# The sum of a row's two magnitudes, ahead of the reciprocal that narrows x, made by GpSimd and not by VectorE

## The chip, the cores and the metric

One NeuronCore of a Trainium2 chip runs the whole program. The metric is the device time of one execution in microseconds (us). Three timed runs of the kernel before gave 1456.22, 1456.29 and 1456.98; the median is 1456.29.

## What is computed

```python
cs = np.cumsum(x, axis=1)                      # x: 8 x 2048 x 2048, float32
diff = cs - (cs shifted by one row, zeros first)
return np.matmul(diff, w).astype(np.float32)   # w: 2048 x 2048, float32
```

The differences of the running sums are x again, so the kernel computes x w: 16384 rows of x, each 2048 long, by a 2048 x 2048 matrix.

## The kernel before

The 16384 rows are cut into 128 tiles of 128 rows. The first four tiles (0 to 3) are multiplied plainly in bf16 while the weights are still coming in (L275, matmuls into eight PSUM banks, one for each row tile and 512 columns). All the others are multiplied in f16 by fewer products than the plain way: x and w are cut into quadrants, sums and differences of quadrants are formed by VectorE, and seven products of half the size take the place of eight. Tiles 4 to 7 use one level of this (`group_plain`), tiles 8 to 11 use two levels in part (`group_half`), and 29 groups of four tiles use two levels, in an order written out by hand (`ORDER`), whose entries name a step and the group that it belongs to. Every engine has its own queue and works it off in the order in which the program was recorded: `after(engine, ...)` keeps the recorded order on each engine. An instruction that waits holds up all that stands behind it on its engine.

So that f16 can be used, every row of x is scaled by its own size, and every product is scaled back. For each of the 124 tiles t from 4 on the steps are:

- `load`: SP fetches the tile in two halves into F.
- `weigh` (L123, ScalarE): for each half the sum of |x| / 4000 along the row goes to column 0 or 1 of a small tile `of` (128 x 8). In the profile this is an ACTIVATE with a following ACTIVATION_READ_ACCUMULATOR, which delivers the sum.
- `scale_of`: column 2, m = max(sum 0 + sum 1, TINY) (L139, VectorE), then column 3, s = 1 / m (L141, VectorE).
- `unit_of` (L147, GpSimd): column 4, u = m times uw, where uw is the scale of the weights. It is used much later, when products are written out.
- `narrow` (L158, ScalarE): x times s to f16, for each half.
- `turn` (L171, SP): a transposing DMA of each half into the tiles x, which TensorE loads as stationary operand.

The products leave PSUM through `keep` (L581, ScalarE) and `add` (L584, VectorE), both scaled by u. VectorE forms the sums of quadrants of x (L544) and of w (L382, L457, L536, L541, L937).

At the head of the program, when the last weights are in, comes this: VectorE forms the largest |w| of each partition (L366), GpSimd reduces that over the partitions (L367, a PARTITION_ALL_REDUCE), and then GpSimd issues seven output DMAs of the plain rows (L285). VectorE turns the result into the weights' scale (L369, L371) and begins to scale the weights to f16: `block(B11, ...)`, `block(B21, ...)`, `block(B12, ...)`, one L382 for each of 8 pieces. Between these blocks stand the `scale_of` of tiles 4, 6 and 5:

```python
for k in range(4):
    block(B11, 0, 0, k, "dve")
weigh(PLAIN); scale_of(PLAIN); unit_of(PLAIN)      # tile 4
for k in range(4, KH):
    block(B11, 0, 0, k, "dve")
narrow(PLAIN); turn(PLAIN); finish_row(0)
for k in range(4):
    block(B21, 1, 0, k, "dve")
weigh(PLAIN + 2); scale_of(PLAIN + 2); unit_of(PLAIN + 2)
finish_row(1)
```

`finish_row(r)` gives TensorE the last plain matmuls of row tile r (L275) and ScalarE the two copies out of its PSUM banks (L295). After the plain rows TensorE does one product that was left over, in the bank that the first copy of row tile 1 empties (`left_over(bank(2))`, L400, 16 matmuls, with all of B11 and B21), and then the products of tiles 4 to 7 (L554).

Of the kernel before, what the change touches and what calls it, by code (L numbers as in the profile page):

```python
# [10 lines left out]
def kernel(  # L11
# [6 lines left out]
    nc = tc.nc  # L18
# [12 lines left out]
    ADD = mybir.AluOpType.add  # L31
    SUB = mybir.AluOpType.subtract
    MUL = mybir.AluOpType.mult
    MAX = mybir.AluOpType.max
# [5 lines left out]
    TINY = 1e-34  # L40
# [45 lines left out]
    def after(engine, ask):  # L86
        if engine in last:
            with tc.issue_after(last[engine].ins):
                said = ask()
        else:  # L90
            said = ask()
        last[engine] = said[-1] if isinstance(said, tuple) else said
        return said
# [38 lines left out]
    def scale_of(t):  # L132
        if t < END:
            m2 = sums_of.pop(t)
            m, s, u = (m2[:, i : i + 1] for i in (2, 3, 4))
            scales[t], unit[t] = s, u
            after(
                "dve",
                lambda: nc.vector.tensor_scalar(m, m2[:, :1], m2[:, 1:2], TINY, ADD, MAX),  # L139
            )  # L140
            after("dve", lambda: nc.vector.reciprocal(s, m))  # L141
            sizes[t] = m
# [37 lines left out]
    with ExitStack() as head:  # L180
# [232 lines left out]
        for k in range(4):  # L413
            block(B11, 0, 0, k, "dve")
        weigh(PLAIN)
        scale_of(PLAIN)
        unit_of(PLAIN)
        for k in range(4, KH):
# [4 lines left out]
        for k in range(4):  # L423
            block(B21, 1, 0, k, "dve")
        weigh(PLAIN + 2)
        scale_of(PLAIN + 2)
        unit_of(PLAIN + 2)
        finish_row(1)
# [15 lines left out]
        for k in range(5, KH):  # L444
            block(B12, 0, 1, k, "dve")
        scale_of(PLAIN + 1)
        unit_of(PLAIN + 1)
        narrow(PLAIN + 1)
# [837 lines left out]
```

## Time and profile before

| | |
|---|---|
| median of three timed runs | 1456.29 us |
| profiled execution: its span, first to last instruction | 1455.0 us |
| instructions | 20120 |
| busy: TensorE / VectorE / ScalarE / GpSimd | 1441.1 / 1333.3 / 967.5 / 48.6 us |
| L139 on VectorE | 124 times, 206 ns each |
| L141 on VectorE | 124 times, 164 ns each |
| L147 on GpSimd | 124 times, 281 to 1896 ns, mean 370 |

The span is that of one profiled execution. The page gives no other time of that execution; the median of the runs stands 1.3 us above the span. Engines are named PE (TensorE's matmuls), PEld (its weight loads), DVE (VectorE), ACT (ScalarE), POOL (GpSimd) and SP (the engine that issues most DMAs). In a row of the timeline stand the start in us from the span's start, the time in us, the engine, line and operation, output and inputs, how many instructions the row merges, and in square brackets how long the engine was idle before and what ended that. In a row of groups the number before the bar is the count, and behind it stand the busy time and the mean ns of one.

### The profile page before, as it was taken

To read this page: it belongs to the slowest core of one execution; us is meant where nothing else is said; L and a number is where in the kernel's file an instruction comes from. 1 tells how busy PE (TensorE), PEld (TensorE's weight loads), DVE (VectorE), ACT (ScalarE), POOL (GpSimd) and SP (SyncE) were. 2 spreads that over 40 slices of the span, in tenths; PEclk is the share of its full clock that TensorE was granted. 3 is DMA by queue.
4 is the path that set the end of the run, shared out by engine and by line. 5 is a ranking of instruction groups with operands and counts; after the bars stand their busy time and mean duration, and the time that the engine had idled before them with its cause. 6 is when DMAs were issued, how large, how long until landed. Compare 5 with 4: busy or idle time off the path is not lost.

```text
span 1455.0 us, 20120 instructions
## 1 busy us (share of the span) xinstructions
PE 1441.1 (99%) x6673; PEld 652.6 (45%) x6679; DVE 1333.3 (92%) x2302; ACT 967.5 (66%) x1446; POOL 48.6 (3%) x136
## 2 busy tenths in 40 slices
PE   8999999999999999999999999999999999999998
PEld 3444444444444444444444444444444444444443
DVE  7998899999999999999999999999999999999998
ACT  5887656676666666667666667766666766666662
POOL 0111000000000000000000000000000000000000
PEclk9999999999999999999999999999999999999999
DMA  9999868898888998878998888998878898888983
GB/s 360 367 240 299 236 171 234 248 246 232 234 237 237 248 253 230 235 236 233 260 241 233 231 228 240 260 238 241 225 235 247 247 233 239 226 244 246 253 203 123
DMA packets 377752, 351.59 MB, mean 242 GB/s; under 512 B 274800, under 2 KB 274800, under 8 KB 377520
## 3 DMA queue, kind: packets, MB, share of 16 engines
q1 hardware_dynamic: 377088, 348.47, 84.9%
q0 software_dynamic: 560, 1.84, 0.3%
q8 instruction: 52, 0.85, 0.2%
q14 instruction: 52, 0.43, 0.1%
HBM read 150.99 MB, written 134.22 MB: 196 GB/s over the span
## 4 chain that ended last, share of the span: by engine, by line
PE 96%; DMA 2%; DVE 1%; issue 0%; ACT 0%; SPq 0%; DVEq 0%; ACTq 0%
PE b L573 61%; PE b L554 32%; PE b L275 2%; DMA W<-in_w_dram 1%; DMA W<-in_x_dram 1%; DVE c L584 1%; ACT wb L259 0%; PE b L400 0%; DVE x L544 0%; SPq L219 0%; DVE b L1030 0%; DVE flow L937 0%; DVE inner L544 0%; DVE W L541 0%; ACT c L581 0%
## 5 line engine op out<-in xcount | busy, mean ns | idle before, releaser
L584 DVE SCALAR_TENSOR_TENSOR c<-b,of,c 128x512 f32<-128x512 f32 x790 | 574.1, 747 | 74.3 <-PE b L573 64.3
L554 PE MATMUL b<-W,x 128*128 128x512 f16 x2144 | 506.6, 379 | 0.0
L581 ACT ACTIVATE c<-b,of 128x512 f32<-128x512 f32 x492 | 312.6, 680 | 230.9 <-PE b L573 113.3
L573 PE MATMUL b<-W,x 128*128 128x512 f16 x1892 | 452.4, 379 | 0.8 <-ACT b L1023 0.7
L158 ACT ACTIVATE F<-F,of 128x1024 f16<-128x1024 f32 x246 | 282.2, 1147 | 174.8 <-DVE of L141 172.6
L573 PEld LDWEIGHTS <-x 128*128 128x128 f16 x2488 | 243.4, 98 | 295.3 <-issue 2.7
L554 PEld LDWEIGHTS <-x 128*128 128x128 f16 x2144 | 209.8, 98 | 253.0 <-DVE x L544 0.2
L123 ACT ACTIVATE waste<-F 128x1024 uint8<-128x1024 f32 x246 | 259.3, 1054 | 4.6 <-DMA F<-in_x_dram 2.5
L573 PEld LDWEIGHTS <-inner 128*128 128x128 f16 x1648 | 161.2, 98 | 195.6 <-issue 1.3
L573 PE MATMUL b<-W,inner 128*128 128x512 f16 x944 | 242.2, 379 | 0.9 <-DVE b L1030 0.9
L544 DVE TENSOR_TENSOR x<-x,x 128x1024 f16<-128x1024 f16 (+1 forms) x388 | 226.6, 584 | 3.3
L573 PE MATMUL b<-flow,x 128*128 128x512 f16 x588 | 150.9, 379 | 0.0
L573 PE MATMUL b<-inner 128*128 128x512 f16 x472 | 121.1, 379 | 0.0
L937 DVE TENSOR_TENSOR flow<-W 128x2048 f16<-128x2048 f16 x87 | 105.8, 1216 | 0.0
L1030 DVE TENSOR_TENSOR b<-b,c 128x512 f32<-128x512 f32 x116 | 80.6, 695 | 13.9 <-PE b L573 13.9
L147 POOL TENSOR_SCALAR of<-of,uw 128x1 f32<-128x1 f32 x124 | 43.6, 370 | 1306.7 <-DVE of L139 704.1
L937 DVE TENSOR_TENSOR flow<-W,inner 128x2048 f16<-128x2048 f16 x58 | 70.8, 1220 | 0.0
L1023 ACT COPY c<-b 128x512 f32<-128x512 f32 x58 | 33.4, 576 | 51.3 <-PE b L573 51.3
L275 PE MATMUL b<-wb,xP 128*128 128x512 bf16 x234 | 57.0, 395 | 5.3 <-ACT wb L259 3.9
L544 DVE TENSOR_TENSOR inner<-x 128x512 f16<-128x512 f16 x117 | 49.4, 422 | 2.9 <-DMA x<-F 0.9
L1023 ACT COPY b<-b 128x512 f32<-128x512 f32 x87 | 51.2, 588 | 0.5 <-PE b L573 0.5
L544 DVE TENSOR_TENSOR inner<-x,inner 128x512 f16<-128x512 f16 x117 | 49.2, 421 | 2.0
(67 smaller groups left out, 530.0 us busy)
## 6 DMA issues: line engine op xcount, KB each, us to landing
F<-in_x_dram SPq DMA_DIRECT2D x246, 512.0 KB, 5.1
out_dram<-c SPq DMA_DIRECT2D x492, 256.0 KB, 3.0
W<-in_w_dram SPq DMA_DIRECT2D x32, 512.0 KB, 9.6
W<-in_x_dram SPq DMA_DIRECT2D x16, 256.0 KB, 7.2
x<-F SPq DMA_TRANSPOSE x246, 3.4
out_dram<-o POOLq DMA_DIRECT2D x5, 256.0 KB, 4.1
out_dram<-o SPq DMA_DIRECT2D x5, 256.0 KB, 3.5
xP<-in_x_dram SPq DMA_DIRECT2D x1, 1024.0 KB, 5.1
```

The costliest lines, as they stand in the source:

```text
L123: lambda: nc.scalar.activation(waste, where[t][i], ABS, scale=1.0 / ROW, accum_out=sums_of[t][:, i : i + 1],),
L147: after("pool", lambda: nc.gpsimd.tensor_scalar(u, m, uw, None, MUL))
L158: lambda: nc.scalar.activation(narrowed(t)[:, ds(i * NH, NH)], where[t][i], COPY, scale=s),
L275: lambda: nc.tensor.matmul(ps[r][n], xP[:, r, ko, :], wb[h, ko][:, ds(n * NB, NB)], start=(ko == 0), stop=(ko == KO - 1),),
L544: after("dve", lambda: nc.vector.tensor_tensor(dst.all, p.all, q.all, op))
L554: said = nc.tensor.matmul(to[n], a[k], b[k][:, n, :], start=(first and k == 0), stop=(k == KH - 1), skip_group_check=True,)
L573: said = nc.tensor.matmul(to, a[k], b[k], start=(first and k == 0), stop=(k == 3), skip_group_check=True)
L581: after("act", lambda: nc.scalar.activation(c, p, COPY, scale=u))
L584: after("dve", lambda: nc.vector.scalar_tensor_tensor(c, p, u, c, MUL, ADD))
L937: after("dve", lambda: nc.vector.tensor_tensor(in_twos(flow), x, y, op))
L1023: after("act", lambda: nc.scalar.copy(c, p))
L1030: after("dve", lambda: nc.vector.tensor_tensor(t, p, s, ADD))
```

## The change

L139 goes from VectorE's queue to GpSimd's. What it computes, its operands and its place in the program are the same.

```diff
             after(
-                "dve",
-                lambda: nc.vector.tensor_scalar(m, m2[:, :1], m2[:, 1:2], TINY, ADD, MAX),
+                "pool",
+                lambda: nc.gpsimd.tensor_scalar(m, m2[:, :1], m2[:, 1:2], TINY, ADD, MAX),
             )
             after("dve", lambda: nc.vector.reciprocal(s, m))
```

GpSimd's queue at the head, behind the output DMAs of the plain rows (`o`). The ISA row is the pair that the profile names MODIFY_POOL_CONFIG; `of` is the small tile of sums and scales.

```order
 L285 DMA out_dram<-o_120 128x512
 L285 DMA out_dram<-o_124 128x512
-L147 ISA
-L147 TENSOR_SCALAR of<-of,uw 128x1 x124
+L139 ISA
+L139 TENSOR_SCALAR of<-of 128x1
+L147 TENSOR_SCALAR of<-of,uw 128x1
```

The configuration and the first L139 stand where the configuration and the first L147 stood, behind the seven DMAs. Before, the first L147 waited for VectorE's L139; now L139 waits for ScalarE's sums, and L147 for L139.

VectorE's queue at the same place, from the weights' scale on. W are the weights.

```order
 L371 RECIPROCAL uinv<-uw 128x1
 L382 TENSOR_SCALAR W<-W,uinv 128x2x512 x4
-L139 TENSOR_SCALAR of<-of 128x1
 L141 RECIPROCAL of<-of 128x1
 L382 TENSOR_SCALAR W<-W,uinv 128x2x512 x8
-L139 TENSOR_SCALAR of<-of 128x1
 L141 RECIPROCAL of<-of 128x1
 L382 TENSOR_SCALAR W<-W,uinv 128x2x512 x12
```

L139 is gone, and L141 stays where it was, with the scaling of the weights behind it; it now waits for GpSimd.

VectorE's queue in a regular group, at one of the four scales of a group; x and inner are quadrant sums of x.

```order
 L544 TENSOR_TENSOR x_69<-x_69,x_70 128x1024
 L544 TENSOR_TENSOR inner<-x_69 128x512
-L139 TENSOR_SCALAR of<-of 128x1
 L141 RECIPROCAL of<-of 128x1
 L544 TENSOR_TENSOR inner<-inner,x_67 128x512
```

Here too only L139 has left. The queues of TensorE, ScalarE and SP hold the same instructions in the same order.

## The prediction

> **What bounds the kernel now.** I read the page first: busy shares and the chain that ended last, then the costliest groups.
>
> ```profile
> span 1455.0 us, 20120 instructions
> PE 1441.1 (99%) x6673; PEld 652.6 (45%) x6679; DVE 1333.3 (92%) x2302; ACT 967.5 (66%) x1446; POOL 48.6 (3%) x136
> PE 96%; DMA 2%; DVE 1%; issue 0%; ACT 0%; SPq 0%; DVEq 0%; ACTq 0%
> ```
>
> TensorE is busy 1441.1 of 1455.0 us and is 96% of the chain. VectorE's 92% looks close behind, but it is an average. So the next view is the busy time by stretch: the stage in which the weights are turned (76 to 131), the first seven-product groups (131 to 197), and the regular groups.
>
> ```profile
> core 0: us, PE busy (x) PEld busy (x) DVE busy (x) ACT busy (x) POOL busy (x), PEclk, DMA share, GB/s
> 76.00:131.00 55.00, 55.00 (x256) 24.95 (x255) 50.73 (x84) 43.83 (x62) 5.97 (x6) 1.00 1.01 260
> 131.00:197.00 66.00, 64.38 (x296) 28.61 (x294) 58.14 (x95) 39.80 (x61) 5.45 (x4) 1.00 0.76 217
> 197.00:1450.00 1253.00, 1252.57 (x5803) 567.57 (x5801) 1161.10 (x2046) 827.81 (x1258) 29.94 (x112) 1.00 0.85 235
> ```
>
> Behind 197 us TensorE is idle for 0.43 us in all (1253.00 - 1252.57), from 131 to 197 for 1.6, from 76 to 131 for nothing. A microsecond taken from VectorE buys nothing there, and a microsecond by which TensorE is held up at the head is not made good later: it goes onto the end.
>
> **What is removed.** The grouped rows of the moved operation and of the operation that GpSimd does already:
>
> ```profile
> L139 DVE TENSOR_SCALAR of<-of 128x1 f32<-128x1 f32 x124 | 25.6, 206 | 3.4 <-ACT waste L123 3.3
> L147 POOL TENSOR_SCALAR of<-of,uw x124: 281/282/1896, 71.8 to 1414.0; 128x1 f32<-128x1 f32 x124
> L147 POOLq MODIFY_POOL_CONFIG  x2: 37/37/37, 64.1 to 64.1; - x2
> ```
>
> VectorE loses 124 x 0.206 = 25.6 us, but about 111 of the 124 lie behind 197 us (GpSimd's 112 operations in that row are L147, one to each L139), beside a full TensorE. I count them at 0. The limit of the gain is the idle time of TensorE above, 2.0 us, and its stalls there are round trips through VectorE and ScalarE that no L139 lies in; I take nothing of it.
>
> **What is added in the regular groups.** One L139 goes to GpSimd for each row tile, and L141 on VectorE then waits for GpSimd. GpSimd's queue ahead of it holds only L139 and L147 of earlier tiles, so it starts when ScalarE's second sum is read out. The tightest such place in a group of 44 us:
>
> ```profile
> 760.89 0.20 ACT L123 ACTIVATION_READ_ACCUMULATOR waste<-F 128x1 f32 x1
> 763.37 0.21 DVE L139 TENSOR_SCALAR of<-of 128x1 f32<-128x1 f32 x1
> ```
>
> The sums are there at 761.09; VectorE comes to this place at 763.37. GpSimd has 2.28 us, and the longest one-column operation that it shows is 1.90. L141 finds its operand there: 0. If that cover were gone (an L139 of 2.6 us), VectorE would wait some 0.3 us, less than it has won.
>
> **What is added at the head.** Here it is another matter. The timeline of the first scale and what hangs on it:
>
> ```profile
> 59.51 1.48 POOL L285 DMA_DIRECT2D out_dram<-F  x2
> 60.98 3.05 POOL L285 DMA_DIRECT2D out_dram<-o  x5
> ...
> 63.40 0.19 ACT L123 ACTIVATION_READ_ACCUMULATOR waste<-F 128x1 f32 x1
> 63.62 0.21 DVE L139 TENSOR_SCALAR of<-of 128x1 f32<-128x1 f32 x1 [0.76 <-ACT waste L123]
> 63.87 0.16 DVE L141 RECIPROCAL of<-of 128x1 f32<-128x1 f32 x1
> 63.95 5.38 DVE L382 TENSOR_SCALAR W<-W,uinv 128x1024 f16<-128x1024 f32 x8
> 64.06 2.33 ACT L158 ACTIVATE F<-F,of 128x1024 f16<-128x1024 f32 x2 [0.48 <-DVE of L141]
> 65.24 2.75 SPq L171 DMA_TRANSPOSE x<-F  x2
> 66.95 1.07 ACT L295 COPY wb<-b 128x512 f32<-128x512 f32 x2 [0.56 <-PE b L275]
> ...
> 70.06 0.18 ACT L123 ACTIVATION_READ_ACCUMULATOR waste<-F 128x1 f32 x1
> 70.16 0.56 ACT L295 COPY wb<-b 128x512 f32<-128x512 f32 x1
> 70.28 0.21 DVE L139 TENSOR_SCALAR of<-of 128x1 f32<-128x1 f32 x1 [0.96 <-ACT waste L123]
> ...
> 70.61 8.03 DVE L382 TENSOR_SCALAR W<-W,uinv 128x1024 f16<-128x1024 f32 x12
> ...
> 71.80 2.26 POOL L147 TENSOR_SCALAR of<-of,uw 128x1 f32<-128x1 f32 x2 [7.77 <-DVE W L382]
> 72.15 3.62 PE L400 MATMUL b<-W,xP 128*128 128x512 f16 x16
> ```
>
> GpSimd's last output DMA is issued by 64.03. Its first one-column operation waits only for the first L139, over at 63.83, and yet starts at 71.80. Between them stand the two MODIFY_POOL_CONFIG at 64.1, which switch GpSimd from the all-reduce to its ordinary operations. The VectorE row printed as releaser cannot be the cause: this L147 reads neither W nor anything that L382 writes, and VectorE's own pause of 0.96 us ahead of 70.28 let nothing in. I read the 7.7 us as the price of the switch. Before the change nobody needs L147 until the first products are written out. After it the switch stands ahead of L139, and VectorE, ScalarE and TensorE stand behind it. Step by step:
>
> - First L139: starts at 71.80 and not at 63.62. Its time on GpSimd is not in the trace; the bounds are L147's 0.28 and 1.90. I take 0.28, since VectorE stands still and L147's long times lie beside a busy VectorE. With about 0.04 to hand over, L141 starts at 72.12: 8.25 us later.
> - Behind L141 on VectorE are eight L382 (second half of B11, first half of B21): 72.2 to 77.6. Behind the narrowing on ScalarE (L158, now from 72.31, 2.33 us, to 74.64) are the copies of row tile 0, the sums of the next x tile and the copies of row tile 1. From the copy at 66.95 to the one at 70.16 ScalarE needs 3.21 us without a pause; from 74.64 this gives 77.85, and with its 0.56 us 78.41. The pause of 0.56 ahead of 66.95 is used up.
> - That copy empties the PSUM bank into which L400 writes. L400 stands next in TensorE's queue, so nothing passes it: it starts at 78.41 and not at 72.15, **6.26 us later**.
> - What else L400 needs is there. The second L139 starts when the sums are read out at 77.94; L141 follows at 78.26, and the last four L382 of B21 come at 0.67 us each (8.03 / 12), from 79.0 to 81.0. L400 needs the first of them at its 13th matmul, 78.41 + 12 x 0.22 = 81.0 at the earliest. The transposes on SP wait for the narrowing and move by 8.3 us, to 76.3; the first product needs them at 81.9.
> - Later on VectorE runs 7.4 us late (8.25 less the pauses and three L139) against TensorE's 6.26. The supplies that arrived closest before had about 1.2 us to spare, so 0 more.
>
> **The clock of TensorE.** A pause of 6.1 us is longer than any in this trace, but two places show what pauses do. First the start, where the PEclk column has no record and the matmul rows have to be read, and then the end:
>
> ```profile
> 12.47 4.45 PE L275 MATMUL b<-wb,xP 128*128 128x512 bf16 x10 [0.78 <-DVE xP L247]
> 17.57 1.99 PE L275 MATMUL b<-wb,xP 128*128 128x512 bf16 x6
> ...
> 1449.00:1450.00 1.00, 0.57 (x3) 1.00 0.71 264
> 1451.00:1452.00 1.00, 0.00 (x0) 0.89 0.86 324
> 1452.00:1453.00 1.00, 0.00 (x0) 0.50 0.36 137
> ```
>
> The ten matmuls from 12.47 come every 0.43 us, the sixteen of L400 every 0.22; the change falls into the row of 17.57, near 18.2. And after the last matmul (1449.57) the granted clock is 0.50 from 1451.8 on: 2.2 us of idleness do it. So after 6.1 us TensorE restarts at half speed. The nearest price is the start's: 12.47 to 18.2 = 5.7 us at half speed, of which half, **2.8 us**, is lost. Bounds: 0 (the clock holds) and 4.6 (half speed as long as from the first of these matmuls, 9.0 to 18.2).
>
> The Trainium skill, "TensorE: Matmul & The Clock Gate", Part 1, has the clock watched in free-running windows of 3.4 us, halved after an idle window and restored after a busy one; by it the loss would be an estimated 1.7 to 3.4 us, and the drop after 2.2 us here agrees only if a window that is partly idle counts.
>
> **Sum.** Against the profiled execution: 1455.0 + 6.26 + 2.8 = 1464.1 us of span. The median of the runs, 1456.29, stands 1.3 above the span; with it, 1465.4.
>
> The Trainium skill, "GPSIMD Engine Reference", section 2.1, gives about 6 us (5.95) for the load of code at the first call after a MODIFY_POOL_CONFIG; the row here has 7.7, which I use, and with 5.95 the sum would be 1463.7.
>
> **Rivals.**
> - **No switch to wait for (not slower).** The 7.7 us were something that held L147 alone (VectorE's L382 blocking GpSimd, say), and L139 runs at once at 64.1. For it: the page's releaser, and twelve long L147 at the head. Then L141 starts at 64.5, 0.6 us late; ScalarE's pause of 0.56 takes that in, L400 still waits for its own turn at 72.15, and the time is 1456.2. It decides if the first L139 ends before about 65.8: the copy that L400 needs was over at 70.72, 1.4 us early, and with the pause that makes 2 us of cover. Against it: GpSimd stayed idle in VectorE's pause.
> - **The switch without the clock.** Half speed is not entered or is left at once: 1456.3 + 6.3 = 1462.6. Against it: 2.2 us sufficed at the end.
> - **Dearer head.** The first L139 takes 1.9 us, and half speed lasts as at its worst: 1465.4 + 1.6 + 1.8 = 1468.8. For it: L147's first two times are long.
> - **Faster.** VectorE's 25.6 us shorten TensorE's stalls behind 76 us: at most 2.0 us, 1454.3, and only together with the first rival.
>
> **How the numbers follow.** The forecast, 0.70; switch without clock, 0.12; dearer head, 0.06; no switch, 0.10; faster, 0.02. A measurement of this kernel tells 0.2% (2.9 us) from no change. Slower is 0.70 + 0.12 + 0.06 = 0.88, same 0.10, faster 0.02. The range takes in both clock cases and most of the dearer head, and something for a switch that is quicker while VectorE and SP stand still: 1461.0 to 1468.5.
>
> **What would show it.** In the profile after: MODIFY_POOL_CONFIG at 64.1 under L139; the first L139 near 71.8; L141 idle before for some 9 us on GpSimd; L400 near 78.4 with ScalarE's L295 as releaser; L400's mean well over 379 ns, and PEclk 0.5 for a few us behind 75; and from 200 us on the same 44 us per group, with everything shifted by one constant. A first L139 at 64.2 proves the first step wrong; L400's matmuls at 379 ns, the clock's; a shift that grows along the groups, the claim that the regular part costs nothing.

## The result and the profile after

The changed kernel takes 1465.33 us (median of 4 runs, 1464.81 to 1466.29); the kernel before, run beside it, 1456.26 (1456.07 to 1456.98). The ratio is 1.0061 with a 95% interval of 1.0047 to 1.0075: slower by 9.1 us, where 1465.4 was forecast.

The span of the profiled execution is 1463.6 us. Its page:

```profile
span 1463.6 us, 20203 instructions
PE 1441.1 (98%) x6673; PEld 652.1 (45%) x6679; DVE 1311.2 (90%) x2178; ACT 969.9 (66%) x1446; POOL 158.1 (11%) x260
```

TensorE's busy time adds up to the same 1441.1 us, VectorE has 22 us less to do, GpSimd 110 more, and the span has grown by 8.6. That TensorE's two sums agree is chance, since slow matmuls count as busy: up to 72.2 us the profile after has 63.1 us of busy time and the one before 65.3, and the slow matmuls of L400 then add 2.4. Where the 8.6 us lie, the timeline of the head shows:

```profile
63.18 0.19 ACT L123 ACTIVATION_READ_ACCUMULATOR waste<-F 128x1 f32 x1
71.99 0.31 POOL L139 TENSOR_SCALAR of<-of 128x1 f32<-128x1 f32 x1 [7.96 <-issue]
72.34 0.16 DVE L141 RECIPROCAL of<-of 128x1 f32<-128x1 f32 x1 [9.48 <-POOL of L139]
72.42 5.37 DVE L382 TENSOR_SCALAR W<-W,uinv 128x1024 f16<-128x1024 f32 x8
72.54 2.33 ACT L158 ACTIVATE F<-F,of 128x1024 f16<-128x1024 f32 x2 [9.17 <-DVE of L141]
...
77.96 0.56 ACT L295 COPY wb<-b 128x512 f32<-128x512 f32 x1
78.15 0.30 POOL L139 TENSOR_SCALAR of<-of 128x1 f32<-128x1 f32 x1 [4.90 <-ACT waste L123]
78.48 0.17 DVE L141 RECIPROCAL of<-of 128x1 f32<-128x1 f32 x1 [0.69 <-POOL of L139]
78.58 6.00 PE L400 MATMUL b<-W,xP 128*128 128x512 f16 x16 [6.49 <-ACT wb L295]
```

The configuration of GpSimd now stands under L139:

```profile
L139 POOLq MODIFY_POOL_CONFIG  x2: 37/37/37, 64.1 to 64.1; - x2
```

The sums are ready at 63.37, and the first L139 starts 8.6 us later, with "issue" as the reason for GpSimd's pause: nothing that the profile records was missing. VectorE waits 9.48 us for it, ScalarE 9.17 us for VectorE, and L400 6.49 us for the copy that empties its bank. L400 itself then needs 6.00 us for the 16 matmuls that took 3.62.

The windows around the restart give the clock (columns: stretch, its length, PE busy, granted clock, DMA share, GB/s), and those behind it, with all engines, what became of the rest (shifted by the 8.8 us of the head):

```profile
75.00:78.00 3.00, 0.00 (x0) 0.77 1.19 207
78.00:83.00 5.00, 4.42 (x11) 0.50 0.89 288
83.00:84.00 1.00, 1.00 (x6) 0.78 0.95 357
84.00:85.00 1.00, 1.00 (x6) 1.00 1.23 298
```
```profile
84.80:139.80 55.00, 55.00 (x256) 24.95 (x255) 49.03 (x77) 42.81 (x60) 9.96 (x12) 1.00 0.97 254
139.80:205.80 66.00, 64.43 (x296) 28.69 (x294) 57.33 (x91) 40.15 (x61) 5.88 (x10) 1.00 0.76 217
205.80:1458.00 1252.20, 1252.20 (x5802) 567.49 (x5800) 1140.40 (x1933) 829.90 (x1258) 134.74 (x223) 1.00 0.86 235
```

TensorE restarts at half clock and has its full clock back within the slice from 83 to 84. From 84.8 on every stretch is what it was: 55.00 of 55.00 busy, then 64.43 of 66 (64.38 before), then a full TensorE. The loss lies wholly ahead of 85 us. In the chain the first product of tile 4 (L554) begins at 84.58 and not at 75.76: 8.8 us.

### The profile page after: what moved, and what is told of

It reads as the page before. It is cut to its first block, busy times and chain, and to the rows that moved or that the text cites. A ratio compares the mean times of both kernels' runs of the same rounds, so it can differ in the third digit from the quotient of the medians.

```text
span 1463.6 us, 20203 instructions
## 1 busy us (share of the span) xinstructions
PE 1441.1 (98%) x6673; PEld 652.1 (45%) x6679; DVE 1311.2 (90%) x2178; ACT 969.9 (66%) x1446; POOL 158.1 (11%) x260
## 4 chain that ended last, share of the span: by engine, by line
PE 93%; DMA 4%; issue 1%; DVE 1%; ACT 0%; POOL 0%; SPq 0%; POOLq 0%; DVEq 0%
PE b L573 61%; PE b L554 33%; DMA W<-in_w_dram 2%; DMA W<-in_x_dram 2%; DVE c L584 1%; PE b L400 0%; POOL out_dram L285 0%; SPq L253 0%; SPq L219 0%; ACT wb L295 0%; ACT waste L123 0%; DVE wmax L262 0%; ACT F L158 0%; DVE b L1030 0%; ACT c L581 0%
## 5 line engine op out<-in xcount | busy, mean ns | idle before, releaser
L554 PE MATMUL b<-W,x 128*128 128x512 f16 x2144 | 506.6, 379 | 0.0
L554 PEld LDWEIGHTS <-x 128*128 128x128 f16 x2144 | 209.7, 98 | 253.0 <-DVE x L544 0.2
L139 POOL TENSOR_SCALAR of<-of 128x1 f32<-128x1 f32 x124 | 96.8, 780 | 1198.4 <-ACT waste L123 1190.5
L147 POOL TENSOR_SCALAR of<-of,uw 128x1 f32<-128x1 f32 x124 | 57.2, 473 | 3.7
L544 DVE TENSOR_TENSOR inner<-inner,x 128x512 f16<-128x512 f16 x117 | 49.5, 423 | 2.1
```

What stands on the lines that cost most here:

```text
L139: lambda: nc.gpsimd.tensor_scalar(m, m2[:, :1], m2[:, 1:2], TINY, ADD, MAX),
L147: after("pool", lambda: nc.gpsimd.tensor_scalar(u, m, uw, None, MUL))
L544: after("dve", lambda: nc.vector.tensor_tensor(dst.all, p.all, q.all, op))
L554: said = nc.tensor.matmul(to[n], a[k], b[k][:, n, :], start=(first and k == 0), stop=(k == KH - 1), skip_group_check=True,)
```

## The experiments

Two theories were in question beside the forecast. The **switch theory** is the forecast's: the reconfiguration of GpSimd behind the all-reduce holds its first ordinary operation for 7.7 us. The **output DMA theory** says that GpSimd is still at work on the seven DMAs that it issued. The **hand-over theory** says that every reciprocal now waits a little for GpSimd, 124 times. Each kernel is told by its difference from the changed one; its line numbers can be up to 17 higher, or one lower.

### Only the first L139 on GpSimd

```diff
-            after("pool", lambda: nc.gpsimd.tensor_scalar(m, ...))
+            name, by = ("pool", nc.gpsimd) if t == PLAIN else ("dve", nc.vector)
+            after(name, lambda: by.tensor_scalar(m, ...))
```

> Only the first row tile's L139 (tile 4) is on GpSimd, the other 123 stay on VectorE. Switch theory: the switch of GpSimd's configuration stands ahead of this one instruction and holds it to about 72 us, so the whole loss is there: first L139 near 72.0, L400 near 78.6 and at half speed, time 1465 (1464 to 1467). Rival, hand-over: each L139 on GpSimd costs the same small wait on its way to VectorE, so 1/124 of the 9 us is left: 1456.4.

Measured: 1465.22 us, ratio 1.0059 (1.0044 to 1.0074). One instruction of the 124 carries the whole loss. Its rows (the moved line is L140 here, L400 is L401):

```profile
72.48 0.31 POOL L140 TENSOR_SCALAR of<-of 128x1 f32<-128x1 f32 x1 [8.05 <-issue]
79.07 6.18 PE L401 MATMUL b<-W,xP 128*128 128x512 f16 x16 [7.15 <-ACT wb L296]
```

The hand-over theory would have left 0.1 us; it falls.

### All but the first on GpSimd

```diff
+            name, by = ("pool", nc.gpsimd) if t > PLAIN else ("dve", nc.vector)
...
```

> The first L139 is back on VectorE, the other 123 are on GpSimd. Switch theory: the switch now stands ahead of the first L147 and of the second L139, which is wanted at 70.3 and comes at about 72.5, so the second reciprocal is some 2 us late; the copy that L400 needs stands ahead of it in ScalarE's queue, and of the last four pieces of B21 the last is late by 0.3 us at most. L400 near 72.2 to 72.6, full speed, time 1456.0 to 1457.0. Rival, hand-over: 123/124 of the loss stays: 1465.

Measured: 1458.66 us, ratio 1.0016 (1.0007 to 1.0024): 2.1 us slower than the kernel before (1456.57), where 0 to 0.5 was expected. The mechanism was there, its size was not. The timeline (L400 is L401, L409 is L410, L554 is L555):

```profile
72.44 0.30 POOL L148 TENSOR_SCALAR of<-of,uw 128x1 f32<-128x1 f32 x1 [7.87 <-issue]
72.73 0.31 POOL L140 TENSOR_SCALAR of<-of 128x1 f32<-128x1 f32 x1
73.07 0.16 DVE L142 RECIPROCAL of<-of 128x1 f32<-128x1 f32 x1 [3.98 <-POOL of L140]
...
75.93 0.38 PE L401 MATMUL b<-W,xP 128*128 128x512 f16 x1 [0.29 <-DVE W L383]
...
84.53 6.20 PE L555 MATMUL b<-W,x 128*128 128x512 f16 x28 [0.45 <-ACT x L410]
```

The second reciprocal waits 3.98 us for the same switch and comes 2.5 us later than before. The gaps between matmul starts that were not there before add up to 2.1 us: 0.8 in L400 for the pieces of B21, 0.6 where a product waits for L400's bank to be emptied, 0.3 at the product with S1 and 0.4 at 98. I had counted the first of these alone. The agreement with 2.1 us is loose: the profiled span is 1.7 us longer than before (1456.7 for 1455.0).

### No switch

```diff
-        whole_max = nc.gpsimd.partition_all_reduce(uw, wred, P, bass_isa.ReduceOp.max)
+        whole_max = nc.gpsimd.tensor_scalar(uw, wred, TINY, None, MAX)
```

> The kernel after the change with the reduction over the partitions left out: GpSimd takes each partition's own largest weight with an ordinary one-column operation in its place, so that the weights' scale differs by partition and the output is not the product; everything else stays, the seven output DMAs ahead of the first L139 too. Switch theory: with no other kind of operation before it there is no switch at 64 us; the first L139 runs right behind the DMAs, near 64.1 to 64.4, L400 near 72.2 at full speed, time 1456 to 1457. Rival, output DMAs: GpSimd is still at work on the DMAs that it issued up to 64.0, their last packets go out at 67.3, and holds its next operation until 72: time stays at 1465.

Measured: 1456.76 us, ratio 1.0001 (0.9992 to 1.0010). There is no MODIFY_POOL_CONFIG at 64 us, and with all 124 L139 on GpSimd and all seven DMAs ahead of them the loss is gone:

```profile
60.68 3.06 POOL L285 DMA_DIRECT2D out_dram<-o  x5
...
63.77 0.32 POOL L139 TENSOR_SCALAR of<-of 128x1 f32<-128x1 f32 x1
64.12 0.16 DVE L141 RECIPROCAL of<-of 128x1 f32<-128x1 f32 x1 [1.57 <-POOL of L139]
...
71.93 3.62 PE L400 MATMUL b<-W,xP 128*128 128x512 f16 x16
```

L139 starts as soon as the last DMA is issued. The output DMA theory falls. The rival of the prediction in which VectorE's L382 block GpSimd falls by the changed kernel itself: there VectorE stood still for 9.48 us, and L139 did not start before 71.99.

### The switch begins sooner

```diff
-        with tc.issue_after(whole_max.ins):
-            for c, rows, columns in done:
-                put(c, rows, columns)
+        for c, rows, columns in done:
+            after("sp", lambda: put(c, rows, columns, nc.sync))
```

> The kernel after the change, with the seven output DMAs of the plain rows issued by SP and not by GpSimd, so that the switch begins right behind the all-reduce at 59.7 instead of 64.1. Switch theory: the first L139 starts near 67.5, 4.4 us sooner than in the kernel after; L400 near 74.2 instead of 72.1, a pause of some 2 us; with what VectorE and ScalarE are then behind, 1459.5 if TensorE keeps its clock over the shorter pause, up to 1461.5 if it does not. Rival, output DMAs: with no DMA work on GpSimd the first L139 runs at 63.4 and the time is 1456.3.

Measured: 1459.40 us, ratio 1.0020 (1.0011 to 1.0030); the lower end of what the switch theory expected.

```profile
L139 POOLq MODIFY_POOL_CONFIG  x2: 83/83/83, 59.0 to 59.0; - x2
```
```profile
66.59 0.31 POOL L139 TENSOR_SCALAR of<-of 128x1 f32<-128x1 f32 x1 [7.53 <-issue]
...
73.18 3.61 PE L399 MATMUL b<-W,xP 128*128 128x512 f16 x16 [1.59 <-ACT wb L295]
```

With no DMA of GpSimd's own in the way the switch still takes 7.5 us. It counts from the configuration and not from the all-reduce: in the changed kernel 4.4 us of DMA issue lie between the two, and the pause behind them is no shorter for it. TensorE's pause is now 1.6 us, and the 16 matmuls take 3.61 us: this pause does not cost the clock. The rest of the 3.0 us above the kernel before (1456.45) comes later, above all here, where TensorE waits for the copy that empties L400's bank (L409 is L408, L554 is L553):

```profile
84.53 7.07 PE L553 MATMUL b<-W,x 128*128 128x512 f16 x32 [0.83 <-ACT x L408]
```

### Two more switches

```diff
-                put(c, rows, columns)
+                last["pool"] = put(c, rows, columns)
+        after("pool", lambda: nc.gpsimd.tensor_scalar(idle[:, :1], wred, TINY, None, MAX))
+        after("pool", lambda: nc.gpsimd.partition_all_reduce(idle[:, 1:2], idle[:, :1], P, ...))
         done = []
```

> The kernel after the change with two more switches ahead of the first L139: behind the output DMAs GpSimd does an ordinary one-column operation, an all-reduce and only then L139; their results are not used. Switch theory: three switches stand ahead of L139 instead of one; if each takes 7.9 us as the first does, L139 starts near 88.5, 16.4 us later than in the kernel after, and the time is 1465.3 + 16.4 = 1481.7; the half speed at the restart is lost once only. If the switch to the all-reduce is free and only the one back costs, 1473.6. Rival, output DMAs: two small operations more, 1466.

Measured: 1478.91 us (2 runs), ratio 1.0154 (1.0134 to 1.0173), 13.6 us above the changed kernel, between the two sizes that were expected. Both directions cost, and not the same:

```profile
71.94 0.25 POOL L376 TENSOR_SCALAR idle<-wred 128x1 f32<-128x1 f32 x1 [7.97 <-issue]
77.96 0.38 POOL L379 PARTITION_ALL_REDUCE idle<-idle  x1 [5.77 <-issue]
85.23 0.31 POOL L140 TENSOR_SCALAR of<-of 128x1 f32<-128x1 f32 x1 [6.89 <-issue]
...
91.81 6.29 PE L408 MATMUL b<-W,xP 128*128 128x512 f16 x16 [19.74 <-ACT wb L296]
```

To the ordinary operations 8.0 and 6.9 us, to the all-reduce 5.8. L139 starts 13.2 us later than in the changed kernel, and so does L400. The half clock is paid once: L400 takes 6.29 us after a pause of 19.7, hardly more than after 6.5.

### TensorE's pause filled

```diff
-        finish_row(3)
+        for ko in range(KO - KQ, KO):
+            plain(1, 3, ko)
+        for i in range(28):   # nil is a tile of zeros
+            after("pe", lambda: nc.tensor.matmul(
+                ps[3][i % 2], nil, wb[1, KO - 1][:, ds(i % 2 * NB, NB)], start=False, ...))
+        plain_out(1, 3)
```

> The kernel after the change with 28 more matmuls in TensorE's pause, between the last plain matmul and L400, which add zero to the sums of the last plain row tile; 28 x 0.216 = 6.0 us of work in a pause of 6.5. Clock theory: TensorE is never idle long enough, L400 starts near 78.6 as before and runs at full speed (mean 379 ns): 2.4 us less than the kernel after, 1462.9 (1462.4 to 1463.5). Rival: L400 and the first products are slow for want of operands, not for the clock: 1465.3 as without the fill.

Measured: 1464.24 us, ratio 1.0055 (1.0041 to 1.0068): 1.1 us less than the changed kernel, not 2.4; the runs of the two kernels overlap (1464.02 to 1465.05, and 1464.81 to 1466.29). The clock did what was expected (L400 is L403, L409 is L412, L554 is L571):

```profile
78.44 3.61 PE L403 MATMUL b<-W,xP 128*128 128x512 f16 x16 [0.62 <-ACT wb L298]
...
89.08 0.67 ACT L412 ACTIVATE x<-b,uw 128x512 f32<-128x512 f32 x1
89.80 5.56 PE L571 MATMUL b<-W,x 128*128 128x512 f16 x25 [0.83 <-ACT x L412]
```

L403 starts where L400 started and takes 3.61 us and not 6.00. But TensorE is now early for what comes behind: until 89.8 it waits for the copy L412, which empties the bank of the left-over product and stands behind the narrowing of tile 5. Matmuls start 1.0 us late there, and 0.1 us more is lost later. In the changed kernel the slow matmuls had covered that. In the kernel before, the same copy is this row:

```profile
81.23 0.67 ACT L409 ACTIVATE x<-b,uw 128x512 f32<-128x512 f32 x1
```

It ended at 81.90, and the matmul that takes over the bank, the 33rd of those that start at 75.60 every 0.216 us, began at 82.5: 0.6 us of cover. In this run the copy comes 7.85 us later than there and the first of these matmuls 6.3 us later (81.89 for 75.60), 1.6 us against 0.6.

### The fill, and that copy ahead of the narrowing

```diff
+        left_over(bank(2))
         scale_of(PLAIN + 1)
         unit_of(PLAIN + 1)
         narrow(PLAIN + 1)
...
-        left_over(bank(2))
```

> The fill of TensorE's pause as in fill_pause, and in addition the copy out of the left-over product's bank (the first ScalarE instruction behind L400) stands ahead of the narrowing of tile 5 in ScalarE's queue and not behind it. With the fill alone TensorE gains 2.4 us of clock and loses 1.0 us again at 88.6, where the product that takes over this bank waits for that copy. Theory: the stall of 1.0 us goes; about 0.5 us of it comes back at the product that needs S1, since VectorE is 7.8 us late and TensorE 6.1; time 1463.7 (1463.1 to 1464.0). Rival: that stall is not the copy's place but the narrowing itself or its operands: no change, 1464.2.

Measured: 1464.83 us, ratio 1.0056 (1.0042 to 1.0070). This was a miss: the stall at L412's bank is gone, but nothing is won. (These runs are from another chip, on which the kernel before took 1456.74.) The next one has grown in its place (L560 is the sum S1):

```profile
96.79 0.69 DVE L560 TENSOR_TENSOR S<-x,x 128x1024 f16<-128x1024 f16 x1 [0.63 <-issue]
...
97.54 3.63 PE L570 MATMUL b<-W,S 128*128 128x512 f16 x16 [0.96 <-DVE S L560]
```

Matmuls start 1.1 us late here. VectorE stood for 0.63 us ahead of this sum, which it had not done with the fill alone; without that wait the stall would be the 0.5 us that was expected. The edit also puts the output DMA of the copy ahead of the transposes of tile 5 in SP's queue, and the sum reads those; that this is the cause was not tried apart. The profiled run's head was also 0.7 us later. So the copy's place made the first stall; of the next one 0.5 us fit VectorE's lateness, and the cause of the other 0.6 stays open.

### GpSimd in the regular groups only

```diff
+            name, by = ("pool", nc.gpsimd) if t >= PLAIN + 12 else ("dve", nc.vector)
...
```

> The first twelve row tiles keep L139 on VectorE as before the change; from tile 16 on, in the regular groups, it is on GpSimd. Theory: there GpSimd has its operands some 2 us or more before VectorE comes to the reciprocal, and TensorE is full: 1456.2 to 1456.6, no difference that can be measured. Rival, VectorE as the bound: 25 us less work on VectorE bring more than 0.2%, below 1453.5. Rival, hand-over: each of the 112 reciprocals waits for GpSimd, above 1459.

Measured: 1456.71 us, ratio 1.0001 (0.9992 to 1.0010): no difference. The window of the regular groups, and VectorE's reciprocal (L142 here), whose idle list is empty:

```profile
197.00:1450.00 1253.00, 1252.36 (x5802) 567.48 (x5800) 1141.01 (x1934) 830.30 (x1258) 134.60 (x223) 1.00 0.85 235
```
```profile
L142 DVE RECIPROCAL of<-of x124: 150/154/166, 63.9 to 1412.9; 128x1 f32<-128x1 f32 x124
its engine sat idle before it (us, times) until:
who waited for it (us, times):
```

VectorE is relieved of 20 us (1161.10 to 1141.01) and no reciprocal waits, but TensorE was and is full: the 0.64 us that are missing of 1253.00 lie behind its last matmul, which ends at 1449.36. In the changed kernel eight reciprocals wait for L139, 14.4 us in all, the last of them at 154.5; in the regular groups none does. None of these kernels is faster than the kernel before.

## Why the prediction was right, step by step

- **The bound.** TensorE full in the regular groups, so nothing won from VectorE: shown by the regular groups alone on GpSimd (1.0001). TensorE is even fuller than the prediction has it. The 0.43 us that it reads as idle time behind 197 us lie behind the last matmul, which ended at 1449.57 in a window that ran to 1450; the limit of a gain was 1.6 us and not 2.0.
- **The start of the first L139.** Forecast 71.80, profile 71.99. That the switch is the cause, and not the DMAs, is shown by the kernel without the all-reduce (63.77, no loss); that it is not VectorE, by VectorE's idleness up to 72.34.
- **Its time and the hand-over.** Forecast 0.28 and 0.04 us, profile 0.31 and 0.04; the reciprocal at 72.34 and not 72.12.
- **The chain through ScalarE to L400.** Forecast 78.41, profile 78.58; the pause is 6.49 us, for 6.26 that L400 was to be late. That this one instruction carries the loss is shown by the kernel with only the first L139 on GpSimd.
- **The clock.** Forecast 2.8 us lost, measured 2.4 (L400's 6.00 against 3.62); shown by the filled pause, in which L400 is back at 3.61. The size was estimated from one stretch at the start, and the drop from one pause of 2.2 us at the end. The drop was safe to forecast: in the ten profiles the granted clock fell between 2.1 and 4.9 us after the last matmul, and this pause is 6.5.
- **"0 more" for the supplies behind.** True of the sum, but by luck: for a reason that the prediction did not give. It had VectorE 7.4 us late against TensorE's 6.26, 1.1 us apart, and 1.2 us of cover. In the filled pause, at full clock, stalls of 1.1 us show up, since the copy out of L400's bank had 0.6 us of cover and was held up 1.6 us more than TensorE. The slow matmuls hide these stalls, so of the 2.4 us of half clock some 1.3 are its own. Taking it away brought the median from 1465.33 to 1464.24, which is 1.1 us, and the start of the profile's last matmul from 1457.8 to 1456.4, which is 1.4; the spread of the runs is as large as that.
- **The sum.** The head moved the first product by 8.8 us (forecast 9.1), and a pause of TensorE of 0.2 us at 196.5 is no longer there: span 1463.6 for 1464.1. The 1.3 us by which the prediction went from span to median compare different executions. Each run of the changed kernel stands 2.2 us above its own span, and each run of the kernel before 1.7 to 1.8 (21 runs), which nothing in the traces explains. The errors cancel, and that the median came within 0.1 us is luck.
- **The rivals.** The one without a switch is refuted; a restart without the clock loss too, since the granted clock is 0.50; the dearer head did not come (the first L139 took 0.31 us), and nothing got faster.

## What to carry to other kernels

Before an operation is moved to a quieter engine, look at what that engine does just before the operation's first use: here the 112 moves in the regular groups were free, and the first one stood behind a reconfiguration of 7.96 us with three engines waiting. Leaving that one on VectorE brought back all but 2.1 us, since the next one then stood behind it. Ask of a gap that cost nothing so far ("idle, waits for nothing shown") what it would cost with something urgent behind it. And when terms of a loss overlap in time, as a slow clock and late supplies do, taking one away returns less than its own size.

## What the runs showed of the hardware

- GpSimd's pause behind MODIFY_POOL_CONFIG was 7.5 to 8.1 us from the all-reduce to ordinary operations at the head (nine kernels), 6.9 in another place, and 5.8 the other way. It was about the same beside a busy VectorE (7.77 in the kernel before) and an idle one (7.96 in the changed kernel).
- A pause of TensorE of 1.6 us left the granted clock at 1.00. After pauses of 6.5 and 19.7 us it restarted at 0.50, and the 16 matmuls behind took 6.00 and 6.29 us for 3.62. The full clock came back 4.9 us after the restart in the changed kernel, 5.2 with only the first L139 moved (L400 6.18 us) and 5.4 with two more switches. The changed kernel's runs spread over 1.5 us; whether the clock's moment of return does that was not tried.
- A one-column operation on GpSimd took 0.31 us beside an idle VectorE. Where VectorE scaled weights (L382) it took up to 2.22 in the changed kernel, the longest of L139 there; that VectorE's work is the cause was not tried apart:

```profile
L139 POOL TENSOR_SCALAR of<-of x124: 286/404/2217, 72.0 to 1417.8; 128x1 f32<-128x1 f32 x124
84.52 2.22 POOL L139 TENSOR_SCALAR of<-of 128x1 f32<-128x1 f32 x1 [5.16 <-ACT waste L123]
```

VectorE waited 0.20 us for this one.
